# A hybrid attention layer on one Trainium2 core: the sums of weight blocks for the seven products move from GpSimd to VectorE

## The chip, the core and the metric

The kernel runs on one core of a Trainium2 chip: a systolic TensorE (PE) for matmuls, whose weight loads run in parallel (PEld), VectorE (DVE), ScalarE (ACT), GpSimd (POOL), SyncE (SP), which here only issues DMAs, and 16 DMA engines. Each engine works through its own list of instructions in order; semaphores tie the lists together. The metric is the device time of one execution in microseconds (us), as the median of several runs; lower is better. Before the change it is 1388.78 us, median of 3 runs (1386.71 to 1389.49).

## The reference

One layer for 1024 new tokens of a prompt and 64 tokens of a running stream, model width 1024, all in fp32. One input projection feeds a sliding-window attention (16 heads, 4 key heads, keys of the own chunk of 64 and of two chunks before) and a gated delta-rule recurrence (8 heads); both outputs are gated, added, projected and normalised:

```python
qa, ka, va, za, qkv_b, a_b, b_b, z_b, g_a, g_b = in_projection(x, w_in)   # x @ w_in
qa, ka = partial_rope(...), partial_rope(...)
oa = window_attention(qa, ka, va, attn_sinks)     # softmax with a sink per head
y_a = (oa * silu(za)) @ w_o_attn
qkv_c = silu(causal_conv(qkv_b))
ob, s_new = gated_delta_chunked(l2norm(q), l2norm(k), v, g, beta, s0)
y_b = (gated_rmsnorm(ob, z_b)) @ w_o_delta
h = sigmoid(g_a) * y_a + sigmoid(g_b) * y_b
y = layer_norm(ALPHA * x + h @ w_out)
```

The change concerns the columns of `in_projection` for the queries `qa`, for part of `za` and for part of the gates `g_a`, `g_b`.

## The kernel before

**Precision.** fp32 matrices are held as a high part `hi` (fp32r) and a low part `lo`; `split` (lines 86 to 90) makes them: ScalarE copies the raw matrix to `hi` (L87), VectorE subtracts `hi` from it to get `lo` (L90). A product is three matmuls: hi·hi, hi·lo, lo·hi.

**Seven products instead of eight.** For the columns named above the kernel multiplies 2x2 blocks with seven products (`stream`, `product`). A job takes two weight tiles of 128 columns (two DMAs of 512 KB into `wraw`, L329). Their halves along the contraction are the blocks a11, a12 (first tile) and a21, a22 (second tile), each 128x512 elements in SBUF. `weights7` makes four sums of them (L335): s1 = a21 + a22, s2 = s1 - a11, s3 = a11 - a21 (written over a21), s4 = a12 - s2 (written over a12). Then it splits the seven blocks into hi and lo, in buffers called `whi`, `wlo` and `wx`. The first sum needs the second tile alone, s2 to s4 need both. There are 14 such jobs: query tiles and parts of za from about 66 us on, and from about 240 us gate tiles, whose products are woven between the steps of the attention. One job is made ready while the products of the job before it run; the two `wraw` buffers come free as the splits of the last blocks of a job are done, which in turn need weight buffers that TensorE has finished with.

**What else VectorE does there.** In 58 to 95 us it makes and splits the sums of x (`sums_x`, `split_sums`), takes the first projections out of PSUM (L472) and computes the decay gates of the recurrence (`gates`, L488 to L526), whose result `scr` TensorE multiplies with small constant matrices (tile `bg<-scr`). From 240 us it carries the softmax of the attention. A unit of attention is scores (TensorE, two PSUM banks from the five of the pool `bg`), the row maximum `mx` (L704), its negative with the sink, `nm` (L706), and `es` (L707), all on VectorE; the exponentials `P` (ScalarE L713, reading the scores from PSUM); their sum `smm` and the division (L714 to L719, VectorE); the transposes of P into two `bg` banks (TensorE L110), their copy to `PT` (L737, one half on ScalarE, one on VectorE), and the product with the values. Three units are in flight. The second half of a unit's transposes takes a bank from which the exponentials of the next unit read their scores just before.

**The order of the work.** A scheduler arranges the instructions of each engine when the program is built: by a priority (code under `urgent` comes early) and by its own estimates of when operands are ready. TensorE's matmuls are pinned to the order of the code. Once built, the order is fixed: an engine whose next instruction waits for a DMA waits with everything behind it.

Of the kernel before, what the change touches and what calls it, by code (L numbers as in the profile page):

```python
# [54 lines left out]
class Build:  # L55
# [266 lines left out]
    def weights7(self):  # L322
        nc = self.nc
        out = []
        with self.urgent():
            raw = []
            for m in range(2):
                r = self.t(self.wp, [128, KT, 128], "wraw", bufs=2)
                nc.sync.dma_start(r, self.I["w_tiles"][self.wn + m])  # L329
                raw.append(r)  # L330
            self.wn += 2
            a11, a12, a21, a22 = (raw[m][:, 4 * k : 4 * k + 4] for m in range(2) for k in range(2))
            S = self.t(self.ws, [128, 2, 4, 128], "sums")
            s1, s2, s3, s4 = S[:, 0], S[:, 1], a21, a12
            sub = lambda d, x, y, op: nc.gpsimd.tensor_tensor(d, x, y, op)  # L335
            sub(s1, a21, a22, ALU.add)
            sub(s2, s1, a11, ALU.subtract)
            sub(s3, a11, a21, ALU.subtract)
            for i, x in enumerate((a11, a12, s2, s1, s3, a22, s4)):
                if i == 2:  # L340
                    sub(s4, a12, s2, ALU.subtract)
                pool, tag, bufs = ((self.wp, "whi", 2), (self.wp, "wlo", 2), (self.ws, "wx", 3))[(0, 1, 2, 0, 1, 2, 2)[i]]
                w = self.t(pool, [128, KT, 128], tag, F32R, bufs=bufs)
                self.split(w[:, :4], w[:, 4:], x)
                out.append((w[:, :4], w[:, 4:]))
        return out
# [1126 lines left out]
```

## Time and profile before

| | |
|---|---|
| median of 3 runs | 1388.78 us (1386.71 to 1389.49) |
| the profiled execution | 1387.56 us, span 1385.8 us |
| PE busy | 1352.8 us, 98% of the span |
| DVE busy | 987.5 us, 71% |
| ACT busy | 624.3 us, 45% |
| POOL busy | 210.3 us, 15% |
| chain that ended last | PE 77%, DVE 14%, ACT 6% |

Times in the trace are counted from the start of the span. A row of the timeline gives the start, the duration, the engine, the line and the operation, output<-inputs by their names in the program, the shape and how many instructions the row merges; in brackets stands how long the engine was idle before it and what released it. Instructions on DVE and ACT overlap a little: the next one starts somewhat before the end that is shown. Where an instruction waited for several things, the bracket names the one that came last by the profile, and this can be another than the one that held it.

### The profile page before, as it was taken

The numbers are of one execution on the slowest core, as the hardware profiler recorded it, in microseconds if no ns is written. First come the engines' busy times: TensorE is split into PE (matmuls) and PEld (weight loads), VectorE is DVE, ScalarE is ACT, GpSimd is POOL, SyncE is SP. The second block draws the span as 40 slices with busy tenths as digits, with TensorE's granted clock in tenths as the row PEclk, the third lists the DMA queues.
The fourth block names the chain that finished last, engine by engine and source line by source line (L and its number), as shares of the span: only waits on it lengthen the run. The fifth ranks groups of instructions, "written<-read, shape, count | busy, mean of one in ns | idle before, by whom it ended". The sixth has DMA issues, their size and how long they took to land.

```text
span 1385.8 us, 30846 instructions
## 1 busy us (share of the span) xinstructions
PE 1352.8 (98%) x11850; PEld 1265.2 (91%) x11850; DVE 987.5 (71%) x2420; ACT 624.3 (45%) x1764; POOL 210.3 (15%) x365
## 2 busy tenths in 40 slices
PE   8999999999999999999999999999999999999997
PEld 8999999999989899988999889988899889999886
DVE  5888556777767478877796777867789546645675
ACT  5364445555556454356633665256643444323000
POOL 1031322111111023111221213011130100000000
PEclk9999999999999999999999999999999999999999
DMA  8425485766665411200221103210356325564221
GB/s 253 116 95 144 112 183 172 193 170 174 179 173 164 138 58 43 64 33 26 91 76 58 33 24 99 90 54 17 99 189 221 97 66 161 187 208 142 97 93 75
DMA packets 152420, 161.64 MB, mean 117 GB/s; under 512 B 54320, under 2 KB 135856, under 8 KB 151984
## 3 DMA queue, kind: packets, MB, share of 16 engines
q1 hardware_dynamic: 138288, 147.76, 36.1%
q10 hardware_dynamic: 13632, 10.78, 2.5%
q8 instruction: 94, 1.54, 0.5%
q0 software_dynamic: 352, 1.11, 0.2%
q14 instruction: 54, 0.44, 0.1%
HBM read 110.91 MB, written 48.70 MB: 115 GB/s over the span
## 4 chain that ended last, share of the span: by engine, by line
PE 77%; DVE 14%; ACT 6%; issue 3%; DMA 1%; SPq 0%; ACTq 0%; POOL 0%; DVEq 0%
PE pj L107 51%; PE bg L107 21%; PE bg L110 4%; DVE acc L821 2%; ACT whi L87 1%; DVE wlo L90 1%; DVE t2k L924 1%; ACT qs L1015 1%; DVE R L1012 1%; ACT w1k L986 1%; DVE t2k L926 1%; DVE ring L90 1%; ACT acc L819 1%; DVE ring L269 1%; DVE rraw L534 0%
## 5 line engine op out<-in xcount | busy, mean ns | idle before, releaser
L107 PE MATMUL pj<-ring,whi 128*128 128x384 f32 (+2 forms) x2840 | 673.9, 326 | 0.0
L107 PEld LDWEIGHTS pj<-ring,whi 128*128 128x128 f32 x2840 | 476.7, 188 | 9.6 <-issue 8.9
L107 PE MATMUL pj<-ring,wlo 128*128 128x384 f32 (+2 forms) x1672 | 463.8, 321 | 1.8 <-DVE rsh L472 1.5
L107 PEld LDWEIGHTS pj<-ring,wlo 128*128 128x128 f32 x1672 | 286.3, 188 | 6.9 <-issue 4.3
L821 DVE SCALAR_TENSOR_TENSOR acc<-pre,sm,acc 128x384 f32<-128x384 f32 (+1 forms) x216 | 132.3, 618 | 36.9 <-ACT acc L819 31.2
L107 PE MATMUL pj<-ring,wx 128*128 128x272 f32 x756 | 110.0, 291 | 2.8 <-ACT u L364 2.6
L107 PEld LDWEIGHTS pj<-ring,wx 128*128 128x128 f32 x756 | 99.6, 188 | 3.7 <-ACT u L364 3.3
L87 ACT ACTIVATE whi<-wraw 128x1024 fp32r<-128x1024 f32 (+2 forms) x72 | 66.7, 927 | 75.4 <-PE pj L107 41.5
L90 DVE TENSOR_TENSOR wlo<-wraw,whi 128x1024 fp32r<-128x1024 f32 (+2 forms) x58 | 67.5, 1164 | 38.4 <-ACT whi L87 38.1
L107 PE MATMUL bg<-ring,whi 128*128 128x384 f32 (+2 forms) x424 | 87.7, 316 | 4.8 <-ACT ring L87 4.7
L107 PEld LDWEIGHTS bg<-ring,whi 128*128 128x128 f32 x424 | 68.5, 190 | 6.0 <-ACT ring L87 5.3
L107 PE MATMUL pj<-pl,ring 128*128 128x512 f32 (+1 forms) x240 | 70.1, 375 | 0.0
L713 ACT ACTIVATE P<-bg,nm 128x192 f32<-128x192 f32 (+2 forms) x136 | 54.5, 409 | 32.8 <-DVE nm L706 30.5
L107 PE MATMUL bg<-ring,wlo 128*128 128x272 f32 (+2 forms) x296 | 66.0, 308 | 0.0
L1015 ACT ACTIVATE qs<-bg,egs 64x128 f32<-64x128 f32 x128 | 46.5, 363 | 36.6 <-DVE R L1012 34.9
L822 ACT ACTIVATE gt<-acc 128x384 f32<-128x384 f32 (+1 forms) x72 | 36.3, 505 | 49.2 <-DVE acc L821 48.1
L828 DVE SCALAR_TENSOR_TENSOR plb<-gt,acc 128x384 f32<-128x384 f32 (+1 forms) x96 | 46.0, 491 | 14.5 <-ACT gt L822 14.2
L1012 DVE SCALAR_TENSOR_TENSOR R<-bg,negc,t2k 64x128 f32<-64x128 f32 x128 | 44.6, 348 | 16.4 <-PE bg L107 15.2
L1038 DVE SCALAR_TENSOR_TENSOR S<-S,dec,bg 128x128 f32<-128x128 f32 x128 | 38.7, 344 | 20.7 <-PE bg L107 19.2
L819 ACT ACTIVATE acc<-pre,sm 128x384 f32<-128x384 f32 (+1 forms) x72 | 43.0, 597 | 20.0 <-DVE plb L828 7.0
L107 PEld LDWEIGHTS pj<-pl,ring 128*128 128x128 f32 x240 | 44.1, 188 | 8.1
L335 POOL TENSOR_TENSOR sums<-wraw 128x512 f32<-128x512 f32 x14 | 18.7, 1332 | 213.4 <-DMA wraw<-w_tiles 131.2
(284 smaller groups left out, 2291.3 us busy)
## 6 DMA issues: line engine op xcount, KB each, us to landing
wraw<-w_tiles SPq DMA_DIRECT2D x80, 512.0 KB, 3.9
q_d<-qsp SPq DMA_DIRECT2D x32, 256.0 KB, 3.5
keys<-k_d SPq DMA_DIRECT2D x28, 256.0 KB, 4.1
q<-q_d SPq DMA_DIRECT2D x64, 96.0 KB, 2.9
gA_d<-gs SPq DMA_DIRECT2D x32, 136.0 KB, 2.6
plb<-prodA SPq DMA_DIRECT2D x8, 544.0 KB, 4.5
plb<-prodB SPq DMA_DIRECT2D x8, 544.0 KB, 4.9
z<-zA_d SPq DMA_DIRECT2D x16, 256.0 KB, 3.2
```

The lines of the kernel that those rows point to most:

```text
L87: i = self.nc.scalar.activation(hi, raw, AF.Copy)
L90: self.nc.vector.tensor_tensor(lo, raw, hi.bitcast(F32), ALU.subtract)
L107: self.tc.keep_in_program_order(self.nc.tensor.matmul(o, l, r, start=start, stop=stop, skip_group_check=skip))
L110: self.tc.keep_in_program_order(self.nc.tensor.transpose(o, x, self.ident))
L713: nc.scalar.activation(P[:, hf, k], ps[:, k], AF.Exp, bias=nm[:, hf, b : b + 1], scale=0.125, accum_out=sm[:, hf, b : b + 1])
L819: nc.scalar.activation(acc[:, :w], pre[:, 0:w], AF.Copy, scale=cw(0))
L821: nc.vector.scalar_tensor_tensor(acc[:, :w], pre[:, j : j + w], cw(j), acc[:, :w], ALU.mult, ALU.add)
L822: nc.scalar.activation(th[:, :w], acc[:, :w], AF.Tanh, scale=0.5)
L828: nc.vector.scalar_tensor_tensor(o, v(th), 1.0, v(acc), ALU.add, ALU.mult)
L1012: nc.vector.scalar_tensor_tensor(R[HS[h]], ks[HS[h], col[h]], self.negc[HS[h], p, c : c + 1], e["vs"][HS[h], i], ALU.mult, ALU.add)
L1015: nc.scalar.activation(qs[HS[1 - h]], ks[HS[1 - h], col[h]], AF.Copy, scale=self.egs[HS[1 - h], p, c : c + 1])
L1038: nc.vector.scalar_tensor_tensor(Sn[:, h], S[:, h], self.egl[h][:, p, c : c + 1], kv[:, 0:128], ALU.mult, ALU.add)
```

## The change

One line: the four sums of L335 are issued on VectorE instead of GpSimd, 14 jobs of 4, so 56 instructions.

```diff
@@ -332,7 +332,7 @@
             a11, a12, a21, a22 = (raw[m][:, 4 * k : 4 * k + 4] for m in range(2) for k in range(2))
             S = self.t(self.ws, [128, 2, 4, 128], "sums")
             s1, s2, s3, s4 = S[:, 0], S[:, 1], a21, a12
-            sub = lambda d, x, y, op: nc.gpsimd.tensor_tensor(d, x, y, op)
+            sub = lambda d, x, y, op: nc.vector.tensor_tensor(d, x, y, op)
             sub(s1, a21, a22, ALU.add)
             sub(s2, s1, a11, ALU.subtract)
             sub(s3, a11, a21, ALU.subtract)
```

TensorE's order of instructions stays word for word the same. VectorE gets the 56 sums, and the scheduler puts other instructions around them in another order.

VectorE in the first job, about 66 to 74 us before the change; `scr` is the chain of the decay gates (L490, L496, L500, L504), `ring2` the splits of the sums of x, `whi`, `wlo` and `wx` the splits of the weight blocks:

```order
 L269 TENSOR_TENSOR parts_72_510<-ring2_8_103 128x544
+L335 TENSOR_TENSOR sums_138_1072<-wraw_137_1070 128x512
 L90 TENSOR_TENSOR parts_75_517<-ck_34_233,parts_74_516 128x128
+L335 TENSOR_TENSOR sums_138_1072<-sums_138_1072,wraw_136_1068 128x512
+L472 SCALAR_TENSOR_TENSOR rsh_108_880<-rsh_108_880,pj_106_852 128x384
+L335 TENSOR_TENSOR wraw_137_1070<-wraw_136_1068,wraw_137_1070 128x512
+L90 TENSOR_TENSOR wx_141_1083<-sums_138_1072,wx_141_1083 128x512
+L90 TENSOR_TENSOR wx_144_1092<-wraw_137_1070,wx_144_1092 128x512
+L90 TENSOR_TENSOR parts_77_525<-ck_34_233,parts_76_524 128x128
 L490 COPY scr_101_827<-bg_100_825 64x9x8
 L90 TENSOR_TENSOR ring2_107_877<-ring2_5_100,ring2_107_877 128x544
+L90 TENSOR_TENSOR whi_139_1076<-wraw_136_1068,whi_139_1076 128x512
```

The sums and two splits of weight blocks have come ahead of the gates' L490. After one more instruction of VectorE (an L472) the list goes on towards L504, the last of the gates, which stands directly behind the rows shown:

```order
+L90 TENSOR_TENSOR wlo_140_1079<-wraw_136_1068,wlo_140_1079 128x512
 L496 TENSOR_TENSOR scr_101_827<-scr_101_827,sm_28_219 128x68
-L472 SCALAR_TENSOR_TENSOR rsh_108_880<-rsh_108_880,pj_106_852 128x384
+L335 TENSOR_TENSOR wraw_136_1068<-wraw_136_1068,sums_138_1072 128x512
 L509 TENSOR_SCALAR beta_104_844<-beta_104_844 128x68
 L90 TENSOR_TENSOR ring2_110_893<-ring2_1_96,ring2_110_893 128x544
-L90 TENSOR_TENSOR parts_77_525<-ck_34_233,parts_76_524 128x128
 L510 RECIPROCAL beta_104_844<-beta_104_844 128x68
 L90 TENSOR_TENSOR ring2_111_904<-ring2_1_96,ring2_111_904 128x544
+L500 SCALAR_TENSOR_TENSOR scr_101_827<-scr_101_827 128x68
 L90 TENSOR_TENSOR ring2_112_915<-ring2_6_101,ring2_112_915 128x544
```

Four sums, which were not on this engine, and four splits of weight blocks and an L472, which stood behind the gates, now stand ahead of the gates' last instruction.

VectorE in the attention, the job whose weights land at about 387 us: `P_825` is the division of one unit, `mx_839` the row maxima of the next.

```order
 L737 COPY PT_834_5335<-bg_836_5341 128x3x128
 L719 TENSOR_SCALAR P_825_5285<-P_825_5285,smm_821_5264 128x192 x4
+L335 TENSOR_TENSOR sums_903_5719<-wraw_902_5717 128x512
+L335 TENSOR_TENSOR sums_903_5719<-sums_903_5719,wraw_901_5715 128x512
+L335 TENSOR_TENSOR wraw_902_5717<-wraw_901_5715,wraw_902_5717 128x512
 L704 TENSOR_REDUCE mx_839_5366<-bg_843_5370 128x2
 L704 TENSOR_REDUCE mx_839_5366<-bg_844_5371 128x2
```

Three sums now stand between the division of one unit and the maxima of the next; the first of them waits for the second weight tile (`wraw_902`).

The same place in the job before 280 us:

```order
 L719 TENSOR_SCALAR P_508_3569<-P_508_3569,smm_504_3548 128x192
+L335 TENSOR_TENSOR sums_593_4042<-wraw_592_4040 128x512
 L704 TENSOR_REDUCE mx_521_3649<-bg_525_3653 128x2
+L335 TENSOR_TENSOR sums_593_4042<-sums_593_4042,wraw_591_4038 128x512
+L335 TENSOR_TENSOR wraw_592_4040<-wraw_591_4038,wraw_592_4040 128x512
 L704 TENSOR_REDUCE mx_521_3649<-bg_526_3654 128x2
 L706 SCALAR_TENSOR_TENSOR nm_522_3650<-mx_521_3649,nsink_29_221 128x4
```

Here the first sum stands ahead of both maxima and the next two between them. In the job at about 423 us the three sums stand as at 387 us; at about 317 and 351 us they stand behind `es` and ahead of `smm` of a unit, so ahead of that unit's division, of a copy to `PT` and of the next maxima.

## Rows read from the trace of the kernel before

**Rows 1.** The page's part 1: busy time of each engine, share of the span, number of instructions.

```profile
PE 1352.8 (98%) x11850; PEld 1265.2 (91%) x11850; DVE 987.5 (71%) x2420; ACT 624.3 (45%) x1764; POOL 210.3 (15%) x365
```

**Rows 2.** Busy time by stretch. Columns: the stretch, its length, then PE, PEld, DVE, ACT, POOL busy in us (instructions), the granted clock of TensorE, the DMA share and GB/s.

```profile
66.00:96.00 30.00, 27.78 (x190) 27.10 (x189) 27.53 (x50) 20.48 (x41) 10.10 (x11) 1.00 0.31 96
...
130.00:240.00 110.00, 110.00 (x882) 110.00 (x881) 62.88 (x130) 50.97 (x130) 27.80 (x20) 1.00 0.63 157
240.00:440.00 200.00, 197.58 (x1796) 181.72 (x1795) 148.32 (x436) 113.86 (x416) 30.92 (x24) 1.00 0.66 180
```

**Rows 3.** What TensorE waited for between 66 and 135 us: total us, times, longest.

```profile
PE pj L107 <- ACT u L364: 2.4, 3, 1.7
PE pj L107 <- DVE rsh L472: 1.5, 1, 1.5
PE bg L107 <- ACT u L364: 0.5, 1, 0.5
PE pj L107 <- DVE ring L90: 0.2, 1, 0.2
```

**Rows 4.** The longest row of the same view between 240 and 445 us.

```profile
PE bg L110 <- ACT P L713: 1.8, 3, 0.8
```

**Rows 5.** The view of line 335 (durations in ns, min/median/max), what GpSimd was idle for before it (total us, times), and of the view of the tile `wraw` the time from issue to landing of its DMAs in 60 to 440 us.

```profile
L335 POOL TENSOR_TENSOR sums<-wraw x14: 1284/1312/1502, 68.3 to 423.4; 128x512 f32<-128x512 f32 x14
  DMA wraw<-w_tiles: 131.2, 9
DMA to landing us min/median/max: 3.8/4.3/6.1
```

**Rows 6.** The timeline of GpSimd and VectorE around 121 us, in the third job.

```profile
120.80 1.32 POOL L335 TENSOR_TENSOR sums<-wraw 128x512 f32<-128x512 f32 x1 [19.61 <-DMA wraw<-w_tiles]
...
121.25 1.18 DVE L532 TENSOR_TENSOR rraw<-rraw,cs 128x272 f32<-128x272 f32 x1
122.34 1.52 DVE L90 TENSOR_TENSOR qsp<-rraw,qsp 128x272 fp32r<-128x272 f32 x1
123.79 1.53 DVE L533 TENSOR_TENSOR rsh<-rsh,cs 128x272 f32<-128x272 f32 x1
125.35 1.41 DVE L534 TENSOR_TENSOR rraw<-rraw,rsh 128x272 f32<-128x272 f32 x1
```

**Rows 7.** VectorE by line and shape, 60 to 445 us: busy us, mean ns of one.

```profile
L90 DVE TENSOR_TENSOR wx<-wraw,wx 128x512 fp32r<-128x512 f32 x26 | 17.8, 689 | 9.9 <-ACT wx L87 9.9
L90 DVE TENSOR_TENSOR whi<-sums,whi 128x512 fp32r<-128x512 f32 x14 | 12.9, 921 | 2.1 <-ACT whi L87 1.8
```

**Rows 8.** The timeline of GpSimd, VectorE and TensorE in the first job.

```profile
68.33 1.50 POOL L335 TENSOR_TENSOR sums<-wraw 128x512 f32<-128x512 f32 x1 [1.52 <-DMA wraw<-w_tiles]
...
73.32 0.23 DVE L504 TENSOR_TENSOR scr<-scr 128x68 f32<-128x68 f32 x1
...
82.76 1.28 DVE L90 TENSOR_TENSOR wx<-wraw,wx 128x512 fp32r<-128x512 f32 x2
...
75.21 0.33 PE L107 MATMUL bg<-scr,u 128*128 128x68 f32 x2
```

**Rows 9.** The timeline of VectorE, ScalarE, GpSimd and TensorE around 387 us.

```profile
383.76 1.00 DVE L719 TENSOR_SCALAR P<-P,smm 128x192 f32<-128x192 f32 x4
385.94 1.02 DVE L704 TENSOR_REDUCE mx<-bg 128x2 f32<-128x384 f32 x2 [1.18 <-PE bg L107]
387.00 0.16 DVE L706 SCALAR_TENSOR_TENSOR nm<-mx,nsink 128x4 f32<-128x4 f32 x1
...
387.28 0.42 ACT L713 ACTIVATE P<-bg,nm 128x192 f32<-128x192 f32 x1 [2.33 <-DVE nm L706]
...
387.79 0.41 ACT L713 ACTIVATE P<-bg,nm 128x192 f32<-128x192 f32 x1
...
387.49 1.31 POOL L335 TENSOR_TENSOR sums<-wraw 128x512 f32<-128x512 f32 x1 [20.22 <-DVE es L707]
...
389.05 0.87 PE L110 MATMUL bg<-cf,P 128*128 128x128 f32 x6
```

**Rows 10.** The same kind of rows at the other jobs within the attention: 279, 317, 351 and 423 us.

```profile
279.26 1.28 POOL L335 TENSOR_TENSOR sums<-wraw 128x512 f32<-128x512 f32 x1 [18.20 <-DMA wraw<-w_tiles]
279.91 0.87 PE L110 MATMUL bg<-cf,P 128*128 128x128 f32 x6
...
316.92 1.30 POOL L335 TENSOR_TENSOR sums<-wraw 128x512 f32<-128x512 f32 x1 [20.93 <-DMA q<-q_d]
...
315.23 0.16 DVE L714 TENSOR_TENSOR smm<-smm,es 128x4 f32<-128x4 f32 x1 [2.27 <-ACT P L713]
...
319.65 1.20 DVE L707 TENSOR_TENSOR es<-nm,nsink 128x4 f32<-128x4 f32 x1
...
322.01 0.55 PE L110 MATMUL bg<-cf,P 128*128 128x128 f32 x3 [0.61 <-ACT P L713]
...
350.87 1.48 POOL L335 TENSOR_TENSOR sums<-wraw 128x512 f32<-128x512 f32 x1 [17.75 <-DVE P L719]
...
355.33 0.88 PE L110 MATMUL bg<-cf,P 128*128 128x128 f32 x6
...
423.37 1.28 POOL L335 TENSOR_TENSOR sums<-wraw 128x512 f32<-128x512 f32 x1 [19.59 <-DMA q<-q_d]
...
423.95 0.87 PE L110 MATMUL bg<-cf,P 128*128 128x128 f32 x6
```

## The prediction, before the changed kernel ran

> **What bounds the kernel now.** I read the page's part 1 first: TensorE is busy for 98% of the span [rows 1], so time is won or lost only where it waits. The table by stretch says where the 14 jobs lie: TensorE is idle for 2.2 of the 30 us from 66 to 96, for nothing from 130 to 240, and for 2.4 of 200 us in the attention; the granted clock is 1.00 throughout [rows 2]. The view of waits names what there is to win: 4.6 us in four groups from 66 to 135 us [rows 3] and 1.8 us for the exponentials in the attention [rows 4]. GpSimd is waited for nowhere in these rows. VectorE is busy for 92% of 66 to 96 us, for 57% from 130 to 240 and for 74% in the attention [rows 2]. The view of line 335 is the one that decides: GpSimd sat idle for 131 us, in nine jobs, until a weight tile had landed [rows 5]. It could sit there for nothing. VectorE can't, for it works its list off in order.
>
> **What the work itself costs.** A sum takes 1.31 us on GpSimd [rows 5]. VectorE does a subtraction of the same shape in 0.69 us, and two in a row take 1.28, so one occupies it for 0.6 [rows 7, 8]. 56 sums are 34 us more of VectorE. But GpSimd's sums slow VectorE down: while the four of the third job run, four VectorE instructions on 272 columns take 1.18, 1.52, 1.53 and 1.41 us [rows 6]; scaled by columns from the 0.69 each should take below 0.5, so some 4 us are lost against 2.4 for four sums. Over all jobs a split that often falls beside the sums averages 921 ns and one that doesn't 689 [rows 7]. So VectorE's load stays about the same, and the change is decided by where it stands still.
>
> The Trainium skill ("SBUF — State Buffer", section "Who interferes with whom") says that a VectorE instruction with two SBUF inputs contends with a GpSimd instruction that reads SBUF, and that one of them then fully blocks. The trace agrees [rows 6]. By that rule alone the change only frees VectorE, which is the first rival below.
>
> The skill also has a rule against the change: "Perfetto Trace Analysis", section "Optimizing Scalar/DVE Operations", holds that work may go from a saturated VectorE to another engine, GpSimd included, and adds that the shared port can undo this. By its first half, the three jobs up to 130 us would lose 3 x 2.4 = 7 us; rows 6 show the second half at work, and I charge nothing for load.
>
> **The first job (66 to 90 us).** TensorE needs the gates' `scr` at 75.21; L504 delivers it at 73.55, 1.7 us early [rows 8]. The second weight tile lands at 68.33, when the first sum starts on GpSimd [rows 8]. In the new order VectorE waits for it there, and ahead of L504 stand four sums and four splits more, 8 x 0.6 = 4.8 us, and four shorter instructions that stood behind L504 or were over by 68.33, each below 0.6, 1.4 together by estimate. About 1.1 comes off, because one instruction in this stretch no longer runs beside a GpSimd sum (each in rows 6 lost about that). L504 then ends at 73.55 + 4.8 + 1.4 - 1.1 = 78.65 and TensorE, whose order is unchanged, loses 78.65 - 75.2 = 3.4 us. Its matmuls that follow are queued behind.
>
> A late TensorE no longer meets some of its waits. Those for the L472 that frees a PSUM bank, for a `ring` split and for the first evictions (1.5 + 0.2 + 0.5 = 2.2 us, rows 3) lie in the next 20 us and go; the 2.4 us for later evictions go if VectorE is not late by then, which rows 6 speak for. So the net is between 3.4 - 4.6 = -1.2 and 3.4 - 2.2 = +1.2; I take **-1**, near the end for which the traced slowing speaks.
>
> **130 to 240 us.** VectorE has 47 of 110 us free and TensorE no wait [rows 2]. Five jobs, in which VectorE may stand still for 1 to 2 us each: 0.
>
> **The attention (240 to 440 us).** At 387 us the path is seen in full [rows 9]. Before, VectorE ends the divisions at 384.8, the maxima start at 385.94, `nm` at 387.00, the first exponential at 387.28, the second at 387.79; with its accumulator read it ends 0.5 later and frees the bank for the second half of TensorE's transposes, which start at 389.05 + 0.39 (the first half's step) = 389.44. From the start of the maxima to the free bank are 1.06 + 0.28 + 0.51 + 0.5 + 0.05 = 2.4 us. After, the three sums stand between the divisions and the maxima, and the first can't start before the tile has landed, taken as GpSimd's start at 387.49 [rows 9]. VectorE stands for 2.7 us, then needs 3 x 0.6 and 0.05 between the first two: maxima at 389.36, bank free at 391.75, TensorE loses **2.3**.
>
> The other jobs by the same offsets [rows 10]:
> - 423: sums from 423.37, maxima 425.24, bank 427.65, wanted at 423.95 + 0.39 = 424.34: **3.3**.
> - 279: the first sum at 279.26, then one maximum (0.47), two sums (1.25), the second maximum (0.6), `nm` at 282.2, 1.35 more to the free bank: 283.5 against 279.91 + 0.39 = 280.3: **3.2**.
> - 317: the sums end at 316.92 + 1.87 = 318.8, ahead of `smm`, which was done at 315.23. The division and the copy behind it take 1.7, the maxima start at 320.5, `es` ends at 321.95. Before, `es` was slowed by GpSimd to 1.20 us and ended at 320.85, and TensorE, at 322.01, did wait 0.61 for the exponentials. It is 1.1 later: **1.1**. This row also proves the path: here the bank is already what TensorE waits for.
> - 351: the sums end at 352.74; `smm`, two products with z, four divisions and the copy to `PT` come first, 2.25 us by the steps in rows 9 (0.23 a division) and an estimate of 1.3 for the rest; maxima at 355.0, bank at 357.4 against 355.33 + 0.39: **1.7**.
> - 246: the divisions that follow the sums come in the end no later, because GpSimd no longer slows them: 0, between -1 and +1.
>
> The fourth sum of each job waits for no DMA and stands in the place of GpSimd's slowing: 0. Together 2.3 + 3.3 + 3.2 + 1.1 + 1.7 = 11.6 us. Of the 1.8 us in rows 4, 0.6 is in the 317 account; of the rest I take 0.5 as gone. What is late next: the divisions and transposes of the same units, but TensorE is late by the same amount then, so nothing is added.
>
> Unknown is when the tiles land. A DMA of a tile takes 3.8 to 6.1 us [rows 5]; if each came 2.3 sooner, the five losses fall from 11.6 to about 1.5; if they come a little later, or VectorE doesn't catch up between jobs, to some 16. I take the landings as traced, since the order of TensorE, which frees the buffers, is the same.
>
> **Sum.** -1 + 0 + 11.6 - 0.5 = **+10.1 us**. The profiled execution took 1387.56 us, 1.2 below the median; that gives 1397.7 on it and 1398.9 on the median. I say **1398.0**.
>
> **Rivals.**
> 1. *Faster: only the slowing goes.* If VectorE comes to the first sum after the landing, nothing stands still, and the waits of rows 3 and 4 go without the 3.4 us: 1388.8 - 4.6 - 1.8 = 1382.4 us. It decides at a landing some 2.5 us earlier in the attention. For it: rows 6. Against it: nine of fourteen first sums started the moment the tile was there [rows 5]. Chance 0.08.
> 2. *No change: the stalls are hidden.* VectorE is free for 26% of the attention [rows 2]; if a stall falls where no unit is waiting, only the first job counts: 1387 to 1391 us. Against it: the sums stand ahead of the maxima, and TensorE waited for the exponentials at 322 us already [rows 10]. Chance 0.12.
> 3. *Worse: VectorE doesn't catch up.* A stall pushes `u` and gate evictions back too, the next loads start later, and a job's loss carries over: half as much again in the attention and +1.2 at the start, 1405 us. Against it: 52 us free in 200. Chance 0.08.
> 4. The forecast, 1391.6 to 1403: 0.72.
>
> A measurement of this kernel tells 0.2% (2.8 us) from no change. Slower by over that, rivals 3 and 4: 0.80; within: 0.12; faster: 0.08. The range, 1389 to 1404, leaves out the faster rival, part of the second and the end of the third.
>
> **What would show it.** In the changed profile L335 on VectorE near 0.69 us; idle time of VectorE before it, 2 to 4 us in each job of the attention and named after the `w_tiles` DMA; a TensorE wait near 75 us for `scr` of about 3 us; waits of L110 for `P` of 1 to 3 us at five places; the four waits of rows 3 gone, and VectorE instructions beside the sums at their short times. It is wrong if VectorE has no idle time ahead of the first sums, or if it has and TensorE's waits in 240 to 440 us stay near 2 us.

## The result and the profile after

The changed kernel takes 1405.48 us, median of 4 runs (1401.82 to 1405.88), against 1388.89 us for the kernel before on the same chip: 1.0115 times as long, 95% interval 1.0101 to 1.0129, +16.6 us. The forecast was 1398.0 with a range of 1389 to 1404. The direction was right; the loss was 1.8 times the 9.2 us of the forecast, and the time lies 1.5 us above the range.

The profiled execution took 1405.87 us, span 1403.9: 18.1 us longer than that of before. The page's part 1, which answers to [rows 1]:

```profile
PE 1361.4 (97%) x11850; PEld 1273.9 (91%) x11850; DVE 993.8 (71%) x2476; ACT 627.5 (45%) x1764; POOL 133.4 (10%) x309
```

VectorE has 56 instructions more and is busy for only 6.3 us longer. TensorE has not one instruction more and is busy for 8.6 us longer: its work became slower, which no wait explains. It is also idle for 42.5 us of the span instead of 33.0, 9.5 us longer; the two make the 18.1 us. What it waited for, from 66 to 135 us (first row, against [rows 3]) and from 240 to 445 us (against [rows 4]); total us, times, longest:

```profile
PE bg L107 <- DVE scr L504: 3.4, 1, 3.4
...
PE bg L110 <- ACT P L713: 11.0, 7, 3.5
PE bg L107 <- DVE PT L737: 1.3, 1, 1.3
PE bg L110 <- DVE z L781: 0.6, 1, 0.6
```

All four waits of [rows 3] are gone, and the one for `scr` stands in their place: 3.4 - 4.6 = -1.2. In the attention 12.9 us stand for 2.4 (the 1.8 of [rows 4] and 0.6 for z, which is also in the view of before): +10.5. That is +9.3 us of waits, nearly all of the added idle time, and leaves 8.8 of the 18.1 us.

The busy time by stretch has the rest (columns as in [rows 2]; the granted clock is the third figure from the end). First the stretches of before, then four shorter ones, each begun where a wait ends, and one more of that kind:

```profile
66.00:96.00 30.00, 26.60 (x161) 26.28 (x160) 24.11 (x50) 20.28 (x39) 3.41 (x6) 0.89 0.30 99
130.00:240.00 110.00, 110.00 (x882) 110.00 (x881) 68.89 (x150) 51.53 (x126) 0.00 (x0) 1.00 0.63 156
240.00:440.00 200.00, 187.71 (x1655) 171.58 (x1653) 138.82 (x423) 102.86 (x375) 0.00 (x0) 0.97 0.62 169
79.00:85.40 6.40, 6.34 (x22) 6.35 (x23) 5.11 (x12) 3.97 (x9) 0.54 (x1) 0.50 0.34 115
284.30:290.40 6.10, 6.10 (x28) 6.10 (x29) 2.59 (x9) 1.93 (x7) 0.00 (x0) 0.50 0.48 124
365.80:369.00 3.20, 3.16 (x15) 3.16 (x16) 2.25 (x8) 2.17 (x9) 0.00 (x0) 0.52 0.62 172
440.80:444.00 3.20, 3.19 (x15) 3.19 (x16) 1.82 (x7) 1.34 (x6) 0.00 (x0) 0.50 0.24 84
403.80:410.00 6.20, 6.16 (x57) 5.85 (x59) 4.47 (x15) 2.69 (x9) 0.00 (x0) 1.00 0.40 95
```

In four spells TensorE is fully busy at a granted clock of 0.50 to 0.52, which is 1.2 GHz; before, the clock was 1.00 in all of these stretches. The spell at 365.8 us follows two waits within 3 us, of 1.34 us (for `PT`) and 0.74 us. By half of the busy time in the spells 3.2 + 3.1 + 1.5 + 1.6 = 9.4 us are lost. That is an estimate and a little too high, for TensorE is busy for only 8.6 us longer. The same is seen in single instructions. TensorE's timeline ahead of the wait for `scr` and behind it:

```profile
74.63 0.51 PE L107 MATMUL pj<-ring,whi 128*128 128x384 f32 x2
...
79.06 0.70 PE L107 MATMUL bg<-scr,u 128*128 128x68 f32 x2 [3.40 <-DVE scr L504]
...
82.21 0.84 PE L107 MATMUL pj<-ring,whi 128*128 128x384 f32 x2
```

Two matmuls of one form take 0.51 us before the wait and 0.84 after it, 1.6 times as long. The Trainium skill ("TensorE: Matmul & The Clock Gate", section "Terms") prices the lower clock at the time spent in it, times one less the granted share: half. The trace comes near that: 9.4 us by the rule, 8.6 us of busy time measured.

Since TensorE's order is the same in both kernels, its lateness can be read off single instructions, here first before and then after the change:

```profile
74.34 0.51 PE L107 MATMUL pj<-ring,whi 128*128 128x384 f32 x2
...
128.08 1.78 PE L107 MATMUL pj<-ring,wx 128*128 128x272 f32 x12 [1.67 <-ACT u L364]
```

```profile
128.48 1.68 PE L107 MATMUL pj<-ring,wx 128*128 128x272 f32 x12
...
280.19 0.55 PE L110 MATMUL bg<-cf,P 128*128 128x128 f32 x3
```

Ahead of the wait for `scr` TensorE is 0.3 us later than before (74.63 against 74.34), at 128 us 0.4, and at 280 us 0.3 again (279.91 in [rows 10]). So the wait of 3.4 us and the spell at 1.2 GHz behind it were won back before 130 us: the old waits that went away gave back more than the 4.6 us of idle time in [rows 3]. In this execution the whole loss arises in the attention.

Now VectorE. The view of line 335: durations (ns, min/median/max), and what VectorE was idle for before it:

```profile
L335 DVE TENSOR_TENSOR sums<-wraw x14: 691/692/693, 69.0 to 436.5; 128x512 f32<-128x512 f32 x14
  DMA wraw<-w_tiles: 24.9, 14
```

A sum takes 0.69 us, as forecast, and VectorE stands 24.9 us for the second tile, in all 14 jobs (GpSimd did in nine [rows 5]); 18.1 of them lie in the six stalls from 240 to 440 us. The slowing is gone: in the third job, where [rows 6] have 1.53 and 1.41 us for L533 and L534, they take 0.44, and the splits that took 921 ns on average [rows 7] take as long as the others:

```profile
124.00 0.44 DVE L534 TENSOR_TENSOR rraw<-rraw,rsh 128x272 f32<-128x272 f32 x1
...
126.17 0.43 DVE L533 TENSOR_TENSOR rsh<-rsh,cs 128x272 f32<-128x272 f32 x1
```

```profile
L90 DVE TENSOR_TENSOR wx<-wraw,wx 128x512 fp32r<-128x512 f32 x26 | 17.9, 690 | 11.1 <-ACT wx L87 10.9
L90 DVE TENSOR_TENSOR whi<-sums,whi 128x512 fp32r<-128x512 f32 x14 | 9.7, 691 | 4.7 <-ACT whi L87 4.5
```

The longest wait of the attention, at 280 us, in the timeline of VectorE, ScalarE and TensorE; it answers to the first two rows of [rows 10]:

```profile
276.37 0.31 DVE L719 TENSOR_SCALAR P<-P,smm 128x192 f32<-128x192 f32 x1
280.15 0.69 DVE L335 TENSOR_TENSOR sums<-wraw 128x512 f32<-128x512 f32 x1 [3.48 <-DMA wraw<-w_tiles]
280.76 0.55 DVE L704 TENSOR_REDUCE mx<-bg 128x2 f32<-128x384 f32 x1
281.23 0.68 DVE L335 TENSOR_TENSOR sums<-sums,wraw 128x512 f32<-128x512 f32 x1
281.83 0.68 DVE L335 TENSOR_TENSOR wraw<-wraw,wraw 128x512 f32<-128x512 f32 x1
282.43 0.55 DVE L704 TENSOR_REDUCE mx<-bg 128x2 f32<-128x384 f32 x1
...
283.22 0.42 ACT L713 ACTIVATE P<-bg,nm 128x192 f32<-128x192 f32 x1 [4.49 <-DVE nm L706]
...
284.28 0.90 PE L110 MATMUL bg<-cf,P 128*128 128x128 f32 x3 [3.54 <-ACT P L713]
```

VectorE stands with the maxima behind it, ScalarE has nothing to do until the negated maxima `nm`, and TensorE waits for the exponentials to leave the bank that its transposes want.

### The profile page after: what moved, and what is told of

The parts are those of the page before. It is cut to its first block, busy times and chain, and to the rows that moved or that the text cites. A ratio compares the mean times of both kernels' runs of the same rounds, so it can differ in the third digit from the quotient of the medians.

```text
span 1403.9 us, 30783 instructions
## 1 busy us (share of the span) xinstructions
PE 1361.4 (97%) x11850; PEld 1273.9 (91%) x11850; DVE 993.8 (71%) x2476; ACT 627.5 (45%) x1764; POOL 133.4 (10%) x309
## 5 line engine op out<-in xcount | busy, mean ns | idle before, releaser
L107 PEld LDWEIGHTS pj<-ring,wlo 128*128 128x128 f32 x1672 | 289.3, 190 | 4.5 <-issue 4.3
L87 ACT ACTIVATE whi<-wraw 128x1024 fp32r<-128x1024 f32 (+2 forms) x72 | 66.7, 927 | 72.2 <-PE pj L107 42.5
L1046 ACT ACTIVATE w1k<-plb 128x128 f32<-128x128 f32 x68 | 20.9, 308 | 64.8 <-DVE plb L1044 60.6
```

What stands on the lines that cost most here:

```text
L87: i = self.nc.scalar.activation(hi, raw, AF.Copy)
L107: self.tc.keep_in_program_order(self.nc.tensor.matmul(o, l, r, start=start, stop=stop, skip_group_check=skip))
L1046: nc.scalar.activation(junk, o, AF.Square, accum_out=d["sso"][:, c : c + 1])
```

## The experiments

Theory A: VectorE stands still for the second weight tile, TensorE waits as long as the softmax or the gates are late, and after some of these waits it runs at 1.2 GHz for some us. Theory B: the time follows VectorE's extra work. Theory C: the lower clock has nothing to do with the waits. Where not said otherwise an edit is to the line of the change in the changed kernel; ratios are to the kernel before on the same chip.

**One part of the jobs at a time.** In all three `self.job` counts the jobs, from -1 at the start (set elsewhere), and the line is

```diff
-            sub = lambda d, x, y, op: nc.vector.tensor_tensor(d, x, y, op)
+            self.job += 1; sub = lambda d, x, y, op, e=nc.vector if self.job in (0,) else nc.gpsimd: e.tensor_tensor(d, x, y, op)
```

with `(0,)` for the first job, `range(1, 9)` for the second to ninth and `range(9, 14)` for the last five.

The first job:

> Sums on VectorE in the first of the 14 jobs alone, on GpSimd in the other 13. Theory A (VectorE stands still for the second weight tile, TensorE waits, and after some of its waits it runs at 1.2 GHz for some us): a TensorE wait for scr L504 of 3.4 us, about 3.1 us lost behind it at the lower clock, some 2.2 to 4.6 us of the old waits gone: +2 to +4.3 us, 1391 to 1393. Theory B (the time follows the work that VectorE has more, evenly over 56 sums): 4/56 of +16.6 us, +1.2, 1390. Theory C (the lower clock has nothing to do with the waits): the wait of 3.4 us is there, the granted clock stays 1.00 from 66 to 96 us, -1 to +1.

1387.80 us, ratio 0.9997 (0.9988 to 1.0006): no change. The wait for `scr` is there with 3.1 us and is the only one from 60 to 135 us. The stretches ahead of its lower clock, in it and after it:

```profile
66.00:80.00 14.00, 10.88 (x68) 10.55 (x68) 12.89 (x29) 9.26 (x18) 1.80 (x3) 1.00 0.32 99
80.00:83.70 3.70, 3.70 (x15) 3.70 (x15) 3.62 (x9) 3.33 (x7) 0.54 (x1) 0.54 0.48 141
83.70:96.00 12.30, 12.30 (x93) 12.30 (x93) 9.20 (x16) 7.92 (x15) 2.58 (x3) 1.00 0.26 90
```

The clock fell where this wait is and nowhere else before TensorE's last matmul, so theory C falls. It stayed low for about half as long as in the changed kernel: 1.7 us lost instead of 3.2. By the views 3.1 + 1.7 - 4.6 = +0.2; measured are -0.3, and neither can be told from no change. Theory A's +2 to +4.3 is a miss: its spell was too long, and what the old waits give back was too small.

The second to ninth job:

> Sums on VectorE in the second to the ninth job (about 95 to 246 us), on GpSimd in the first and the last five. Theory A: VectorE has free time there and stands for 1 us at most, no wait of TensorE is added and the clock stays 1.00; of the 4.6 us of waits from 66 to 135 us up to 2.4 go, because VectorE and ScalarE are no longer slowed beside GpSimd's sums: 0 to -2.4 us, 1386.4 to 1388.8. Theory B: 32/56 of +16.6 us, +9.5, 1398.

1385.55 us, ratio 0.9985 (0.9977 to 0.9994), 2.6 us less. The waits of TensorE from 60 to 135 us are

```profile
PE pj L107 <- DVE rsh L472: 1.5, 1, 1.5
PE bg L107 <- ACT u L364: 0.5, 1, 0.5
PE pj L107 <- DVE ring L90: 0.2, 1, 0.2
```

The 2.4 us of waits for evictions in [rows 3] are gone and nothing came for them; the clock is 1.00 everywhere up to 500 us. So on these eight jobs, with 32 of the 56 sums, the change is a gain, and theory B (+9.5) falls for them. The reason in the expectation holds for VectorE alone: in the kernel before, ScalarE's L364 takes 0.38 to 0.43 us throughout, beside GpSimd's sums and apart from them, so ScalarE itself was not slowed.

The last five jobs:

> Sums on VectorE in the last five jobs (about 279 to 437 us), on GpSimd in the first nine. Theory A: waits of TensorE for the exponentials of some 11 us in place of 1.8, and some 6 us lost behind them at the lower clock: +15 to +17 us, 1404 to 1406. Theory B: 20/56 of +16.6 us, +6, 1395. Theory C: the waits alone, +9 to +10.5, 1398 to 1399.

1403.48 us, ratio 1.0115 (1.0095 to 1.0135), and the profiled execution has the waits of the changed kernel in the attention (11.7 us for the exponentials) and three spells at 0.50. The median is 0.5 us below theory A's range, with runs from 1400.9 to 1407.8. Five jobs carry nearly the whole loss.

**The sums later in the order.**

```diff
-            sub = lambda d, x, y, op: nc.vector.tensor_tensor(d, x, y, op)
+            sub = lambda d, x, y, op: self.tc.keep_in_program_order(nc.vector.tensor_tensor(d, x, y, op))
```

> All 56 sums on VectorE as in the changed kernel, but their place in the order tied to TensorE's: a job's sums come only behind the matmuls that stand before them in the code, some us after the second weight tile has landed. The work of VectorE is the same to the instruction. Theory A: VectorE no longer stands for the tile, the wait for scr and the long waits for the exponentials go and the clock stays 1.00: 1383 to 1390. What could go against it in this kernel alone: the sums and splits come in one bunch of some 5 us and late for TensorE's second product. Theory B: the load is the same, so 1405.

1400.67 us, ratio 1.0093 (1.0079 to 1.0107): a miss for theory A's number. VectorE no longer stands for any tile and the wait for `scr` is gone. But the bunch that the expectation names is there, and it comes ahead of the softmax and not only of the second product, for instance ahead of a wait of TensorE of 2.31 us at 345.54; VectorE's timeline:

```profile
338.83 0.68 DVE L335 TENSOR_TENSOR sums<-wraw 128x512 f32<-128x512 f32 x1
...
342.57 0.68 DVE L90 TENSOR_TENSOR wlo<-wraw,wlo 128x512 fp32r<-128x512 f32 x1
343.17 1.01 DVE L704 TENSOR_REDUCE mx<-bg 128x2 f32<-128x384 f32 x2
```

Seven instructions of 0.6 us run ahead of the maxima, 4.3 us in all, about as long as a stall, and four spells at 1.2 GHz follow in this run too. So it doesn't tell stall from load; work that is ready, and stands ahead of the maxima for some 4 us, costs about as much as a wait there.

**Load beside GpSimd's sums.** To the line of the kernel before is added, with `R(i)` half of the i-th tile of x as 128x512:

```diff
+            [nc.vector.tensor_tensor(s2, R(i), R(i + 4), ALU.subtract) for i in range(4)]
```

> The kernel before, with its sums on GpSimd, and beside them in each of the 14 jobs four subtractions of two 128x512 halves of x on VectorE, under the same priority, into the place of s2 before s2 is made; they wait for no DMA and their result is written over. VectorE gets the load of the change (56 instructions of that shape, 34 us) without the stall, and keeps the slowing by GpSimd. Theory A (the stall decides): waits of TensorE for the exponentials below 5 us, clock mostly 1.00, 1389 to 1394. Theory B (the load decides): 1405 or more.

1409.35 us, ratio 1.0150 (1.0136 to 1.0164): theory B's number. But the added instructions write the place of s2, and in the first job GpSimd's own s2 had to wait for the last of them, which VectorE does at 90.61 us:

```profile
91.39 1.67 POOL L335 TENSOR_TENSOR sums<-sums,wraw 128x512 f32<-128x512 f32 x1 [2.26 <-DVE sums L335]
```

In the kernel before, this sum starts at 76.15. The split of `wx` comes behind it, and TensorE waits 4.0 us for that. The added instructions also run beside GpSimd's sums, which the change takes away. That is two things which the change doesn't have. So the next two runs try to take the stall and the load apart without them.

**The stall alone, and the load alone.** To the line of the kernel before is added:

```diff
+            nc.vector.tensor_copy(s2[:, 0, 0:1], a21[:, 0, 0:1])
```

> The kernel before, sums on GpSimd, and in each job one copy of one element per partition of the second weight tile on VectorE, at the places where the change has its first sum: VectorE stands for the tile and does no sum. Theory A (the stall alone decides): most of the +16.6 us, 1398 to 1405. Theory A2 (e5_load: the stall and the sums that follow it lie on one path to the exponentials, which has some 1.4 to 2 us to spare per job, so neither alone costs what both do): by the offsets of rows 9 and 10 without the three sums 1.5 at 279, 0.5 at 387, 1.5 at 423 us, 0 to 1 at the others, and up to 1.6 at the lower clock: +3 to +6, 1391 to 1394. Theory B (load): 1388 to 1389.

In the changed kernel the four sums become, with `R(i)` as above:

```diff
-            sub(s1, a21, a22, ALU.add)
-            sub(s2, s1, a11, ALU.subtract)
-            sub(s3, a11, a21, ALU.subtract)
+            nc.vector.tensor_tensor(s1, R(0), R(4), ALU.subtract)
+            nc.vector.tensor_tensor(s2, R(1), R(5), ALU.subtract)
+            nc.vector.tensor_tensor(s2, R(2), R(6), ALU.subtract)
...
-                    sub(s4, a12, s2, ALU.subtract)
+                    nc.vector.tensor_tensor(s2, R(3), R(7), ALU.subtract)
```

> The changed kernel, whose 56 sums take halves of x, which lie ready, in place of the blocks of the weight tiles (so the four sums of weight blocks are left out, s3 and s4 stand as the blocks they were, and the product comes out as something else): VectorE has the load of the change to the instruction, GpSimd does no sums and slows nothing, and no sum waits for a tile. Theory A: the load is paid by the slowing that is gone: 1383 to 1390. Theory A2: a sum or two ahead of the maxima cost less than the slack: 1385 to 1393. Theory B: the load is all that counts: 1402 to 1406.

The stall alone: 1402.34 us, ratio 1.0097 (1.0077 to 1.0116). The load alone: 1389.36 us, ratio 1.0010 (1.0000 to 1.0020). So 34 us of work on VectorE that waits for nothing, with GpSimd silent, cost 1.3 us, and theory B falls. The scheduler has put these instructions elsewhere, though: in the first job behind the gates (from 85.9 us), and in the attention only those of two jobs stand among the maxima. And 14 copies of 0.15 us each that wait for a tile, at the places of the change's first sums, cost 14.3 us, within theory A's range. VectorE's timeline with the stall alone at the job of [rows 9]:

```profile
397.30 1.00 DVE L719 TENSOR_SCALAR P<-P,smm 128x192 f32<-128x192 f32 x4
402.12 0.15 DVE L335 COPY sums<-wraw 128x1 f32<-128x1 f32 x1 [3.82 <-DMA wraw<-w_tiles]
402.20 1.01 DVE L704 TENSOR_REDUCE mx<-bg 128x2 f32<-128x384 f32 x2
```

Not all of the 14.3 us is the stall. At the job of 317 us in [rows 10] four divisions take, first with the stall alone, then in the changed kernel:

```profile
324.79 3.50 DVE L719 TENSOR_SCALAR P<-P,smm 128x192 f32<-128x192 f32 x4
```

```profile
325.81 1.00 DVE L719 TENSOR_SCALAR P<-P,smm 128x192 f32<-128x192 f32 x4
```

With the stall alone they run beside GpSimd's sums, which the same tile has set going; at 364.45 four take 2.39 us. At these two jobs the run pays for a slowing that the changed kernel doesn't have. At the other three, TensorE waits 1.8, 1.6 and 1.6 us (at 286, 405 and 442 us) where the changed kernel has 3.5, 2.3 and 2.1. So the stall brings a large part of the loss without a sum on VectorE, but how much of each wait in the changed kernel is the stall, and how much the three sums behind it, these runs don't separate. Theory A2 misses the time; of its offsets, 1.5 us at 279 and at 423 fit, and 0.5 at 387 doesn't, where the tile came later (a stall of 3.82 us against 2.52).

TensorE's waits from 240 to 455 us, first of the stall alone, then of the load alone:

```profile
PE bg L110 <- ACT P L713: 9.9, 7, 2.0
PE bg L110 <- DVE z L781: 1.2, 1, 1.2
PE bg L107 <- DVE z L781: 0.9, 1, 0.9
```

```profile
PE bg L110 <- ACT P L713: 6.6, 6, 2.0
```

The load does cost waits in the attention, 6.6 us against 2.4, and earns them back before 135 us, where 1.0 us is left of 4.6; the clock is 1.00 to the end of its work. With the stall alone the waits are 12.0 us there and 5.7 before 135 us, 10.7 more than before, and four spells at 1.2 GHz come on top, each of the shorter kind.

**Matmuls in place of the wait.** In the changed kernel, ahead of the matmul that waits for `scr`:

```diff
-        cols = 4 * NCH
+        cols = 4 * NCH; [self.mm(ps[:, 272:512], self.ring[0][:, 0, :128], self.ring[0][:, 0, :240]) for _ in range(28)]
```

> The changed kernel, with 28 matmuls on 240 columns put into TensorE's order just ahead of the one that waits for scr, into unused columns of its PSUM bank; they take some 3 us in place of most of the wait of 3.4 us, and nothing reads them. Theory A: the wait for L504 is below 1 us, the granted clock stays 1.00 from 66 to 96 us where it was 0.89, and the 3.1 us behind the wait come back: 1402 to 1403 against 1405.5. Theory C (the lower clock has nothing to do with TensorE standing still): the clock falls there as before, 1405 to 1406.

1403.95 us, ratio 1.0086 (1.0056 to 1.0116), too wide to tell; so it was run again beside the changed kernel on one chip.

> The changed kernel once more, beside e12_fill on the same chip: 1402 to 1406.

> The kernel of e6_fill again, whose three used times lay 1396 to 1404 apart and said nothing of 3 us. Theory A: 2 to 4 us below e11_again and no fall of the clock in the first job. Theory C: the same as e11_again.

The changed kernel: 1402.23 us, ratio 1.0099 (1.0082 to 1.0116). With the matmuls: 1401.47, ratio 1.0093 (1.0078 to 1.0108). The busy time from 66 to 96 us, first of the changed kernel in this run, then with the matmuls:

```profile
66.00:96.00 30.00, 26.68 (x161) 26.36 (x160) 24.63 (x50) 19.62 (x38) 3.41 (x6) 0.89 0.32 102
```

```profile
66.00:96.00 30.00, 30.00 (x215) 29.82 (x214) 26.91 (x57) 20.89 (x41) 3.42 (x6) 1.00 0.37 122
```

The gates are as late as before, but TensorE does not stand, and the clock stays at 2.4 GHz. So it is the standing, not the lateness, that brings the clock down: theory A, against C. In time only 0.8 us came of the 3 forecast, and the two intervals overlap. In the attention VectorE stood longer for the last two tiles of this run (3.83 and 3.42 us against 2.33 and 2.09), and TensorE waited longer behind it, 13.7 us in the attention against 10.4; that takes back what the first job gave. Whether an earlier TensorE brings that about, or the landings differ from run to run, wasn't settled.

**A version that beats both.** The first nine jobs on VectorE, the last five on GpSimd, and the first job's sums not under `urgent` (`low` is the priority outside it):

```diff
-            sub = lambda d, x, y, op: nc.vector.tensor_tensor(d, x, y, op)
+            def sub(d, x, y, op): p = self.tc.cur_priority; self.tc.cur_priority = p if self.job else low; (nc.vector if self.job < 9 else nc.gpsimd).tensor_tensor(d, x, y, op); self.tc.cur_priority = self.tc.cur_priority if self.job else p
```

> Sums on VectorE in the first nine jobs, on GpSimd in the last five; those of the first job alone at the lower priority of the code around them, so that the gates' chain L490 to L504 stands ahead of three of its sums. Theory A: no wait for scr over 1 us, the clock stays 1.00, and the waits of rows 3 go further than in e2_mid, where 2.2 us were left: 1383 to 1386. Theory B: 36/56 of +16.6 us, +10.7, 1399.

1382.97 us, ratio 0.9960 (0.9948 to 0.9973): 5.3 us less than the kernel before and 19 to 23 less than the changed one on its two occasions. From 60 to 240 us TensorE waits for nothing at all, and the clock is 1.00. From 240 to 455 us:

```profile
PE bg L110 <- DVE z L781: 1.6, 1, 1.6
PE bg L110 <- ACT P L713: 1.3, 3, 0.6
```

With the condition `self.job < 9 or d is s4` the last five jobs' fourth sum goes to VectorE as well:

> As e7_nine, and of the last five jobs the fourth sum (s4), which needs no fresh tile, on VectorE too. My step 'the fourth sum of each job costs 0' says the time of e7_nine within 1 us, and nearly no idle time of VectorE ahead of it. If load counted, 5 x 0.6 us or more would be added.

1383.10 us, ratio 0.9964 (0.9952 to 0.9977), the same as without. Five sums that wait for no fresh tile cost nothing that shows, in the attention too.

## Why the prediction was right, and where it failed

- *The first job.* The wait is right: L504 was to end at 78.65 and TensorE to lose 3.4 us; L504 ends at 79.00 and TensorE waits 3.40. That it fits to the tenth is luck, since TensorE too came 0.3 us later than before. Of the old waits all 4.6 us went, so the net of waits is -1.2 where -1 was taken. But with the spell at 1.2 GHz and what the old waits gave back, the job cost nothing: the -1 did not come.
- *130 to 240 us: 0.* Right; TensorE is busy for all of it.
- *The attention.* Each wait is right within 1.2 us: 3.5 for 3.2 at 279, 0.9 more than before for 1.1 at 317, 2.1 for 1.7 at 351, 2.3 for 2.3 at 387, 2.1 for 3.3 at 423 us. Their sum, with the old ones set off, is +10.5 against 11.6 - 0.5 = 11.1. The step behind them, "I take the landings as traced", held within 1.3 us, counted from where TensorE stood; at 423 us the tile came 1.0 us sooner, and the wait is 1.2 shorter than forecast. (For tiles that come 2.3 us sooner the five losses would by the prediction's own figures fall to 1.9, not to "about 1.5"; nothing hangs on it.)
- *The sum.* +9.3 us of waits were measured, +10.1 forecast. What failed is the step that carried this sum straight to the time: "TensorE, whose order is unchanged, loses 78.65 - 75.2 = 3.4 us", and so on for each wait, with a clock that "is 1.00 throughout [rows 2]". That row holds for a TensorE that waits for 1.7 us at most. The forecast put waits of 1 to 3.4 us into it and left the clock where it was. A term is missing: the work at 1.2 GHz in the four spells behind the waits, 8.6 us by TensorE's busy time. In the attention alone 10.5 us of waits and, by half of the busy time, 3.1 + 1.5 + 1.6 = 6.2 us at 1.2 GHz make 16.7 of the some 17.8 us that were lost there, against 11.1 forecast. The range didn't have it either; its upper end was built from longer stalls. On the second occasion the changed kernel took 1402.2 us, inside the range, with the same term missing; that the range held there is luck.
- *The work itself.* "I charge nothing for load": right, +1.3 us in the run with the load alone, and the slowing is gone from the rows. Of the two rules weighed in the prediction, that of the Trainium skill ("SBUF — State Buffer", section "Who interferes with whom") fits where nothing stands still: the slowed instructions are back at their short times, and the eight jobs of the middle gain 2.6 us. It is the first rival in a part of the kernel.
- *The rivals.* No change and faster fell as a whole. The third, 1405, comes to the time but not by its mechanism: the losses did not grow from job to job. The second tile of the job at 423 us was asked for at 431.75 instead of 417.50, 14.3 us later, and TensorE was 14.3 us late there itself.
- *By hand once more.* In the stall run the same offsets gave +3 to +6 us without the sums, and it was +14.3. Two terms were missing: again the four spells at 1.2 GHz, some 6 us, and the slowing by GpSimd's sums, by which TensorE waited 1.9 and 2.0 us at 330 and 369 us where 0 to 1 was expected.

## What to carry to other kernels

An engine that works in order should not be given an instruction that waits for a DMA ahead of work that the bottleneck needs, nor a bunch of ready work as long as that wait; an idle engine that waits for the DMA alone is the better place, even at twice the duration and with slowing beside it. Split such a change by stages: it paid where the engine had room and nothing urgent behind the wait, and lost where a chain to the bottleneck stood behind it. And when a forecast puts waits of some 2 us or more into a TensorE that was fully busy, count not only the waits but the time at half clock behind them, of nearly the same size again here (8.6 us beside 9.3).

## What was not expected of the hardware

TensorE worked at the lower clock for some 3 or some 6 us at a time in these runs, with about 1.6 or 3.1 us lost each. Which wait brings one is not told by its length alone: waits of 1.60 us (in the stall run) and 2.06 us (the changed kernel, at 441 us) were followed by a spell, waits of 2.30 us (at 404 us, the last row of the table by stretch) and of 3.24 us (with the matmuls, at 401 us of its first run) by none. The Trainium skill ("TensorE: Matmul & The Clock Gate", section "HAM oscillation — how this bites in real kernels") describes waits for data that bring the clock down again each time. These traces show that waits can bring it down, but not that each does. What decides in the single case wasn't tried. It is a part of another thing that was measured: the changed kernel's median was 1405.5 on one occasion and 1402.2 on the other. The profiled execution of the first has two spells of the longer kind and 12.9 us of waits in the attention, that of the second one such spell and 10.4 us of waits. Why the waits differ is open.
